# A hybrid decoder layer on one core: output ahead of the next joining, sample sums in a bank of their own, fewer DMAs in the inversion, embeddings projected by halves

## The chip, the cores and the metric

One Trainium2 chip, of which the kernel uses one core. The metric is device time in microseconds (us) of one execution. All times here are medians of repeated executions, or belong to the one execution that the profiler recorded.

## What is computed

One decoder layer is applied to a prompt of 1024 tokens and to 8 sequences of 8 tokens each ("the sample"), in float32.

```python
proj = x @ w_in                                   # token shift, RWKV-7 heads and gated-delta heads together
o_a = _rwkv7_mix(proj[..., :A_SHIFT_W], ...)      # 8 heads of 64
o_b = _gated_delta_mix(proj[..., A_SHIFT_W:], ...)# 4 heads of 128, chunks of 64
x = _layer_norm(DN_ALPHA * x + concat(o_a, o_b) @ w_o)
x = _layer_norm(DN_ALPHA * x + _conv_ffn(x))      # w_up (1024 x 5632), conv, silu, w_down (2816 x 1024)
e = _rms_norm(p @ w_ple)                          # per-layer input embeddings
x = x + sigmoid(x @ w_ple_gate) * e
```

Both mixers walk through the prompt in chunks. Within a chunk the recurrence becomes a triangular system (`triangular_solve(eye + Lmat, rhs)` in the reference for the gated-delta heads, the same in form for the RWKV heads), and a state is carried from chunk to chunk. The outputs are the two results and the new states.

## The kernel before

**Big products.** Every product with a weight matrix runs on TensorE (PE) in float32 that is split into two parts: `split` writes the rounded part `hi` on ScalarE (ACT) and the rest `lo` by a subtraction, on VectorE (DVE) or GpSimd (POOL) as its caller says. Three matmuls (hi·hi, hi·lo, lo·hi) of 128x512 add up in one PSUM bank. `wchunk` loads a weight chunk (`wraw`) and splits it into `whi` and `wlo`. There are three buffers of `whi`.

**Banks.** PSUM has 8 banks of 128x512. They are handed out by name: 4 `acc`, 2 `aux`, 2 `scan`. Within a name the banks go round in the order in which the program asks for them. A user that comes later in the program can't have a bank before the users ahead of it have had theirs. The four staging tiles `st` go round in the same way.

**Units.** Mixing is cut into 8 prompt units (half of the prompt `tb`, head group `g`, half of that `h`) and two sample units. A unit has five steps: `prep` (convolution, gates, the triangular matrices `MG` and `MB`), `invert`, `merge`, `scan` (the walk along the chunks, in the `scan` banks) and `mix_out`. `prep`, `merge` and `mix_out` use the `aux` banks.

**Inversion.** `invert` treats the 16x16 diagonal blocks of 24 systems of 64x64. Four DMAs write the matrices to DRAM (`inv_t`), four read the blocks back as 96 rows of 256 (`iN`), 28 short VectorE operations substitute into `iY`, two DMAs write the result and its transpose (`inv_x`, `inv_y`), and 16 read them back as `Dd` and `Dt`. All of these stand on the ACT engine's queue. `merge` then joins the blocks in four rounds of 64x64 matmuls. Each round opens with `touch`, a small matmul `aux<-zeros` that waits for the round's data, in the first two rounds for the DMAs of `Dt` and `Dd`. Behind it VectorE writes `DX` or `Y`.

**Order.** Instructions are put in order by the priority of their place in the program. What stands in `with s.fill()` has a lower priority and fills TensorE while a unit waits ("filler"): the projections of both halves (`proj`), the embeddings (`ple`), `w_o`, `w_up` and `w_down`. The first six column pairs of `proj(0)` stand ahead of `prep` of the first unit, pairs seven and eight (`next(pj)` twice) directly behind its `merge`. The loop over units runs `scan` of unit i with `merge` of unit i+1 woven into it (`ahead`), then `mix_out` of unit i, then `prep` of unit i+2.

**The sample in proj(0).** `proj_pair` multiplies each weight chunk with the prompt (two `acc` banks) and with the sample (a `scan` bank). `sfold` then transposes the sample's result in another `scan` bank and `store_sample` stores it, one pair late: ahead of `store_raw` of the pair that follows. `store_raw` is what empties that pair's two `acc` banks, through `st` tiles.

Of the kernel before, what the change touches and what calls it, by code (L numbers as in the profile page):

```python
# [16 lines left out]
D = 1024  # L17
# [128 lines left out]
class Kern:  # L146
    def __init__(s, ctx, tc, I, O):
        s.tc, s.nc, s.I, s.O = tc, tc.nc, I, O
        s.cp = ctx.enter_context(tc.tile_pool(name="const", bufs=1))
        s.mp = ctx.enter_context(tc.tile_pool(name="main", bufs=1))  # L150
        s.sp = s.mp
        s.ps = ctx.enter_context(tc.tile_pool(name="ps", bufs=4, space=PSUM))
        s.dp = ctx.enter_context(tc.tile_pool(name="dram", bufs=1, space=DRAM))
        s.bad, s.raw, s.rows, s.XW = {}, {}, {}, {}
        s.nbank = {"acc": 4, "aux": 2, "scan": 2}
        s.n = 0
        s.row = None
# [28 lines left out]
    def sbank(s):  # L186
        return s.bank("scan")

# [83 lines left out]
    def setup(s):  # L272
# [44 lines left out]
        for t in (s.Dd, s.Dt, *s.DX):  # L317
# [38 lines left out]
    def load_x(s, src, more=None):  # L356

        x = s.xtiles()
        if not more and not s.late:
            for k in range(0, KT, 2):  # L360
                raw = s.tl([128, D], "X", 3, dt=F32R, pool=s.c0).bitcast(F32).rearrange("p (k t) -> p k t", k=2)
                s.nc.sync.dma_start(raw, src[:, k:k + 2, :])
                s.split(x[k // 2][:, 0], x[k // 2][:, 1], raw, s.nc.vector if k < 4 else None)
            return x
        for k in range(KT):
            raw = s.hraw() if s.late else s.st()
            with s.tc.high_priority() if more and k < 1 else ExitStack():
                s.nc.sync.dma_start(raw, src[:, k, :])
                s.split(*s.xk(x, k), raw, s.nc.vector if more else None)
# [4 lines left out]
    def load_xs(s):  # L374
# [3 lines left out]
        def load(k):  # L378
            ks = slice(k, k + 2)
            s.nc.sync.dma_start(raw[:, ks], s.I["xT"][:, ks, T:T + 64])  # L380
            s.split(x[:, ks, 0, :], x[:, ks, 1, :], raw[:, ks], s.nc.vector)
# [3 lines left out]
    def wchunk(s, src, to=None):  # L385
# [4 lines left out]
        with s.tc.high_priority():  # L390
            s.nc.sync.dma_start(raw[:, :w], src)
            s.split(hi[:, :w], lo[:, :w], raw[:, :w], s.nc.vector)
        return hi, lo

    def proj_group(s, x, xs, wsrc, cuts, sample):

        acc = [s.bank("acc") for _ in cuts]
        sacc = s.sbank() if sample else None
# [42 lines left out]
    def sfold(s, pb, n):  # L441

        b = s.sbank()
# [9 lines left out]
    def proj(s, tb):  # L453
# [8 lines left out]
        if sample:  # L462
            s.store_sample(s.uad[:, 12:14], s.sfold(pb, 2), 2)
            q = s.sbank()
# [481 lines left out]

    def invert(s, sa, sb, small):

# [5 lines left out]
        dT = s.tl([64, 24, 64], "inv_t", 2, pool=s.dp)  # L954
        d1, d2 = (s.tl([96, 16, 16], t, 2, pool=s.dp) for t in ("inv_x", "inv_y"))
        N, Y, tmp = s.iN, s.iY, s.it
        DX = s.DX[0]
        s.DX = s.DX[::-1]
        for h, y, t in s.systems(sa, sb):
            s.uq.dma_start(dT[:, h * nh + y:h * nh + y + t.shape[1], :], t)  # L960
# [11 lines left out]
        s.uq.dma_start(d1[:n], Y[:n])  # L972
        if small:
            nc.gpsimd.memset(DX, 0.0)
            todo = ((DX, d1, 64),)
        else:
            nc.vector.tensor_copy(N[:n], Y[:n].rearrange("p c i -> p i c"))
            s.uq.dma_start(d2[:n], N[:n])
            todo = ((s.Dt, d2, 0), (s.Dd, d1, 0))
        for D, d, w in todo:  # L980
            for h in range(2):
                for k in range(4):
                    rows = slice(64 * h + 16 * k, 64 * h + 16 * k + 16)
                    cols = slice(w * h + 16 * k, w * h + 16 * k + 16)
                    y = k * ns + h * nh
                    if small:
                        s.uq.dma_start(D[rows, :2 * nch, cols], d[y:y + 2 * nch].rearrange("y r t -> r y t"))
                        if h == 0:
                            y += 2 * nch
                            s.uq.dma_start(D[rows, 8:8 + nb, cols], d[y:y + nb].rearrange("y r t -> r y t"))  # L990
                    else:
                        i = s.uq.dma_start(D[rows, :, cols], d[y:y + nh].rearrange("y r t -> r y t"))
                        sa.setdefault("dma", []).append(i.ins)
        sa["DX"] = sb["DX"] = DX

    def merge(s, sa, sb):
# [72 lines left out]
    def scan(s, tb, half, g, st, ahead):  # L1069
# [14 lines left out]
        s.together(a_all(), b_all(), *ahead)  # L1084
# [167 lines left out]
    def banks(s, alt):  # L1252
        return [s.bank(t) for t in (("aux", "aux", "scan", "scan") if alt else ("acc",) * 4)]
# [72 lines left out]
    def transposed(s, xs, i, c0, x, tag, dst=None):  # L1326
# [5 lines left out]
        for k in range(0, KT, q):  # L1332
# [19 lines left out]
            s.tt(lo, u, hi.bitcast(F32), ALU.subtract, s.nc.gpsimd if (k // q) % 2 else None)  # L1352
# [16 lines left out]
    def ple(s):  # L1369
        nc, I = s.nc, s.I  # L1370
        for tb in range(3):
# [12 lines left out]
            for h in range(2):  # L1384
# [6 lines left out]
                def evac(t, b):  # L1391
# [4 lines left out]
                s.dense(2, (lambda i: x[i]) if x else None, lambda i: I["w_ple"][h][:, i, :], evac,  # L1396
                        None if x else (lambda i: xs[:, i]), lambda v: out(8, 64, v))
# [211 lines left out]
    def run(s):  # L1609
# [124 lines left out]
```

## Time and profile before

| | |
|---|---|
| median of 3 runs | 1924.78 us (1918.24 to 1928.16) |
| the profiled execution | 1920.4 us, its span 1918.6 us |
| PE busy | 1831.8 us, 95% |
| DVE busy | 1269.8 us, 66% |
| ACT busy | 918.0 us, 48% |
| POOL busy | 154.7 us, 8% |
| mean granted TensorE clock | 0.989 of full speed |
| DMA | 255.88 MB, mean 133 GB/s |

Busy time counts what an engine executes; the issue of a DMA is not counted. The granted clock is one of two levels, 2.4 GHz (1.00) or 1.2 GHz; a stretch in between has some of each.

### The profile page before, as it was taken

Reading aid. Unit: us, or ns where it says so; the run is one execution under the profiler, and the core shown is the slowest. Engines: PE = TensorE matmul, PEld = TensorE weight load, DVE = VectorE, ACT = ScalarE, POOL = GpSimd, SP = SyncE. Lnnn points to the kernel's source line nnn. Section 1 sums busy time; section 2 is a strip of 40 time slices with the busy share of each in tenths; the row PEclk is TensorE's granted clock in tenths of the full one; section 3 lists DMA queues with packets and bytes.
Section 4 is the critical chain, followed back from the end, with each engine's and each line's share of the span. In section 5 each row is a group of like instructions: output and inputs, shape, how many; then the busy total and the mean of one; then the engine's idle time right before and its main releaser. Section 6 shows DMA issues by size and latency. Waiting matters only on the chain. (4 is left out here: it accounts for less than half of the span.)

```text
span 1918.6 us, 29879 instructions
## 1 busy us (share of the span) xinstructions
PE 1831.8 (95%) x10446; PEld 1463.3 (76%) x10446; DVE 1269.8 (66%) x2748; ACT 918.0 (48%) x1814; POOL 154.7 (8%) x305
## 2 busy tenths in 40 slices
PE   9999999999799798999999999999999999999998
PEld 7878777777567577777887767777787888888877
DVE  4366566758586685877768767666857752455488
ACT  5454447465564744646455435543633332333372
POOL 2000010001000000000000000200212210111000
PEclk9999999999899899999999999999999999999999
DMA  6435342434444365442423446875332222222355
GB/s 216 152 123 153 112 113 89 137 100 133 144 138 145 126 181 163 129 114 82 117 81 112 131 137 194 274 246 200 134 119 92 96 78 83 83 78 79 114 174 165
DMA packets 219126, 255.88 MB, mean 133 GB/s; under 512 B 81848, under 2 KB 117096, under 8 KB 218976
## 3 DMA queue, kind: packets, MB, share of 16 engines
q1 hardware_dynamic: 162040, 246.36, 39.8%
q10 hardware_dynamic: 56936, 7.62, 2.5%
q8 instruction: 82, 1.34, 0.3%
q14 instruction: 68, 0.56, 0.1%
HBM read 200.64 MB, written 53.26 MB: 132 GB/s over the span
## 5 line engine op out<-in xcount | busy, mean ns | idle before, releaser
L190 PE MATMUL acc<-x,whi 128*128 128x512 f32 x2400 | 784.5, 403 | 7.9 <-ACT whi L217 5.1
L220 DVE TENSOR_TENSOR wlo<-wraw,whi 128x512 fp32r<-128x512 f32 (+1 forms) x462 | 323.2, 700 | 343.7 <-ACT whi L217 319.0
L217 ACT ACTIVATE whi<-wraw 128x512 fp32r<-128x512 f32 (+1 forms) x462 | 287.4, 623 | 497.8 <-PE acc L190 169.0
L190 PEld LDWEIGHTS acc<-x,whi 128*128 128x128 f32 x2400 | 429.5, 189 | 89.0 <-issue 7.8
L190 PE MATMUL acc<-x,wlo 128*128 128x512 f32 x1200 | 483.0, 403 | 0.0
L190 PEld LDWEIGHTS acc<-x,wlo 128*128 128x128 f32 x1200 | 226.9, 189 | 54.3 <-issue 6.0
L190 PE MATMUL acc<-whi,X 128*128 128x512 f32 x436 | 145.5, 407 | 9.5 <-ACT st L217 6.2
L217 ACT ACTIVATE st<-acc 128x512 f32<-128x512 f32 (+2 forms) x134 | 77.4, 595 | 62.3 <-PE acc L190 39.2
L190 PEld LDWEIGHTS acc<-whi,X 128*128 128x128 f32 x436 | 81.9, 191 | 29.8 <-ACT st L217 7.2
L190 PE MATMUL acc<-wlo,X 128*128 128x512 f32 x220 | 87.5, 398 | 0.0
L229 DVE SCALAR_TENSOR_TENSOR st<-st,par,st 128x512 f32<-128x512 f32 (+1 forms) x132 | 78.1, 593 | 2.8
L217 ACT ACTIVATE st<-st 128x512 f32<-128x512 f32 x66 | 33.3, 505 | 72.9 <-DVE st L229 68.4
L190 PE MATMUL scan<-whi,X 128*128 128x256 f32 (+2 forms) x208 | 62.4, 335 | 0.0
L217 ACT ACTIVATE tmp<-tmp 128x512 f32<-128x512 f32 (+4 forms) x75 | 40.5, 548 | 30.6 <-DVE tmp L229 22.7
L229 DVE SCALAR_TENSOR_TENSOR st<-st,st 128x512 f32<-128x512 f32 x74 | 40.6, 550 | 19.5 <-ACT st L217 18.6
L190 PE MATMUL scan<-whi,xsm 128*128 128x256 f32 x176 | 49.3, 281 | 2.4 <-ACT st L217 2.4
L190 PE MATMUL scan<-wlo,X 128*128 128x256 f32 (+2 forms) x164 | 51.5, 314 | 0.0
L217 ACT ACTIVATE X<-wraw 128x512 fp32r<-128x512 f32 (+1 forms) x65 | 40.5, 623 | 21.1 <-DMA wraw<-hd 10.7
L506 POOL COPY tail<-st 128x3 f32<-128x3 f32 x52 | 14.6, 283 | 436.6 <-ACT st L217 436.6
L220 DVE TENSOR_TENSOR X<-wraw,X 128x512 fp32r<-128x512 f32 x60 | 43.5, 724 | 9.4 <-ACT X L217 9.3
L217 ACT ACTIVATE tmp<-tmp,par 128x256 f32<-128x256 f32 (+1 forms) x100 | 43.0, 470 | 14.0 <-issue 4.5
L190 PE MATMUL scan<-wlo,xsm 128*128 128x256 f32 x176 | 49.5, 282 | 0.0
(358 smaller groups left out, 3306.9 us busy)
## 6 DMA issues: line engine op xcount, KB each, us to landing
wraw<-w_up SPq DMA_DIRECT2D x176, 256.0 KB
wraw<-w_in SPq DMA_DIRECT2D x112, 256.0 KB
wraw<-w_down SPq DMA_DIRECT2D x98, 256.0 KB
wraw<-hd SPq DMA_DIRECT2D x44, 256.0 KB
wraw<-w_o SPq DMA_DIRECT2D x32, 256.0 KB
wraw<-w_gate SPq DMA_DIRECT2D x32, 256.0 KB
hd<-st SPq DMA_DIRECT2D x22, 256.0 KB
st<-lnv SPq DMA_DIRECT2D x20, 256.0 KB
```

The lines of the kernel that those rows point to most:

```text
L190: i = s.nc.tensor.matmul(out, lhsT=lhsT, rhs=rhs, start=start, stop=stop)
L217: s.nc.scalar.activation(out, in_, f, **kw)
L220: (eng or s.nc.vector).tensor_tensor(out, a, b, op)
L229: s.nc.vector.scalar_tensor_tensor(out, a, sc, b, op0, op1)
L506: s.nc.gpsimd.tensor_copy(s.tails[tb][:, f0 + f, :], st[:, TB - 3:TB])
```

## The change

1. **Order of the loop.** `merge` of unit i+1 is no longer woven into `scan` of unit i. It stands behind `mix_out` of unit i.
2. **Banks.** `acc` has 3 banks, and one bank is named `sum`. The sample's sums in `proj(0)` go to `sum`. Where there is no sample, `fbank` goes round over all four. `sfold` and the sample's gates in `proj(0)` take `aux` banks in place of `scan` banks.
3. **Inversion.** One DMA in place of four reads `iN`. The two results are written as 16x16 blocks on the diagonals of 64x64 systems in DRAM (`inv_dd`, `inv_dt`), in pieces of 64 bytes, and read as whole 64x64 systems with 4 DMAs in place of 16. The space beside the diagonal is set to zero once, by four DMAs at the start.
4. **Splits.** All subtractions of `split` and of the transposing splits run on VectorE, none on GpSimd.
5. **Embeddings.** The two weight chunks of a half are loaded first and kept, and the four token groups of 128 go in two halves, (0, 1) and (2, 3).

```diff
-        s.nbank = {"acc": 4, "aux": 2, "scan": 2}
+        s.nbank = {"acc": 3, "sum": 1, "aux": 2, "scan": 2}
+        s.turn = 0
...
+    def fbank(s, sample=False):
+        if sample:
+            return s.bank("acc")
+        s.turn = (s.turn + 1) % 4
+        return s.bank("acc" if s.turn else "sum")
...
-    def split(s, hi, lo, raw, eng=None):
+    def split(s, hi, lo, raw):
         s.act(hi, raw)
-        s.tt(lo, raw, hi.bitcast(F32), ALU.subtract, eng or s.nc.gpsimd)
+        s.tt(lo, raw, hi.bitcast(F32), ALU.subtract)
...
+        s.dd, s.dt = (s.tl([24, 65 * 64], t, pool=s.dp) for t in ("inv_dd", "inv_dt"))
+        for t in (s.dd, s.dt):
+            for h in range(2):
+                s.uq.dma_start(s.sysrows(t, slice(h, 24, 2)), s.DX[0][64 * h:64 * h + 64, :, 0:64])
...
     def proj_pair(s, x, xs, wsrc):
-        acc = [s.bank("acc") for _ in range(2)]
-        sacc = s.sbank() if xs is not None else None
+        early = xs is not None and not s.late
+        acc = [s.fbank(early) for _ in range(2)]
+        sacc = None if xs is None else s.bank("sum") if early else s.sbank()
...
     def sfold(s, pb, n):
-        b = s.sbank()
+        b = s.sbank() if s.late else s.bank()
...
+    def blocks(s, d, ns):
+        b = d.rearrange("y (k q) -> (y k) q", k=4)[:4 * ns, :16 * 64]
+        return b.rearrange("p (r l) -> p r l", l=64)[:, :, :16]
+
+    def sysrows(s, d, y):
+        return d[y, :64 * 64].rearrange("y (r t) -> r y t", t=64)
...
-        for k in range(4):
-            s.uq.dma_start(N[k * ns:(k + 1) * ns], dT[16 * k:16 * k + 16, :ns, 16 * k:16 * k + 16].rearrange("r y t -> y r t"))
+        s.uq.dma_start(N[:n], s.blocks(dT, ns))
...
-        s.uq.dma_start(d1[:n], Y[:n])
...
+            nc.vector.tensor_copy(N[:n], Y[:n].rearrange("p c i -> p i c"))
+            for X, d, D in ((N, s.dt, s.Dt), (Y, s.dd, s.Dd)):
+                s.uq.dma_start(s.blocks(d, ns), X[:n])
+                for h in range(2):
+                    i = s.uq.dma_start(D[64 * h:64 * h + 64], s.sysrows(d, slice(h, 24, 2)))
+                    sa.setdefault("dma", []).append(i.ins)
...
-                s.touch(bs[0], s.nc.cur_bb.bb.instructions[-1], *(sa["dma"][8 * k:8 * k + 8] if k < 2 else ()))
+                s.touch(bs[0], s.nc.cur_bb.bb.instructions[-1], *sa["dma"][2 * k:2 * k + 2])
...
-        s.together(a_all(), b_all(), *ahead)
+        s.together(a_all(), b_all())
...
-            s.tt(lo, u, hi.bitcast(F32), ALU.subtract, s.nc.gpsimd if (k // q) % 2 else None)
+            s.tt(lo, u, hi.bitcast(F32), ALU.subtract)
...
-                s.dense(2, (lambda i: x[i]) if x else None, lambda i: I["w_ple"][h][:, i, :], evac,
-                        None if x else (lambda i: xs[:, i]), lambda v: out(8, 64, v))
+                W = [s.wchunk(I["w_ple"][h][:, i, :]) for i in range(2)]
+                s.dense(2, (lambda i: x[i]) if x else None, None, evac, None if x else (lambda i: xs[:, i]),
+                        lambda v: out(8, 64, v), parts=((0, 1), (2, 3)) if x else ((),), kept=W)
...
-                    o = s.sample_scan(*u, st[i]) if len(u) == 1 else s.scan(*u, st[i], [s.merge(*st[i + 1][:2])] if len(units[i + 1]) == 3 else [])
+                    o = s.sample_scan(*u, st[i]) if len(u) == 1 else s.scan(*u, st[i])
...
                         s.mix_out(*u, st[i], o)
+                    if i + 1 < len(units) and len(units[i + 1]) == 3:
+                        for _ in s.merge(*st[i + 1][:2]):
+                            pass
```

**The first unit on TensorE.** Before, on PE, from the last transposes of `prep` (`aux_1290<-cst,tmp`) on, and further down at the first two rounds of `merge` (`acc` and `scan<-whi` or `wlo` are filler of `proj(0)`; `aux_1358` to `aux_1390` are `merge`):

```order
L214 MATMUL aux_1290<-cst_83,tmp_1243 128x128 x4
L190 MATMUL scan_2008<-whi_2032,X_135 128x256
L190 MATMUL scan_2008<-wlo_2033,X_135 128x256
L190 MATMUL acc_2006<-x_139,whi_2054 128x512 x2
...
L190 MATMUL acc_2225<-x_139,wlo_2273 128x512
L190 MATMUL aux_1358<-zeros_104 128x8
L190 MATMUL aux_1358<-Dt_120,MG_1188 64x64 x16
L190 MATMUL aux_1359<-Dt_120,MB_1265 64x64 x8
L190 MATMUL scan_2226<-whi_2272,X_135 128x256
...
L190 MATMUL aux_1389<-zeros_104 128x8
L190 MATMUL aux_1389<-Dd_119,DX_35_121 64x64 x16
```

After, on PE, the same stretch, from the same transposes (`aux_1294`) to the third round of `merge`, with nothing left out:

```order
L222 MATMUL aux_1294<-cst_83,tmp_1247 128x128 x4
L198 MATMUL aux_1345<-zeros_104 128x8
L198 MATMUL aux_1345<-Dt_120,MG_1192 64x64 x16
L198 MATMUL aux_1346<-Dt_120,MB_1269 64x64 x8
L198 MATMUL aux_1376<-zeros_104 128x8
L198 MATMUL aux_1376<-Dd_119,DX_35_121 64x64 x16
L198 MATMUL aux_1377<-Dd_119,DX_35_121 64x64 x8
L198 MATMUL aux_1405<-zeros_104 128x8
L198 MATMUL aux_1405<-Y_1343,DX_35_121 64x64 x16
```

No filler is left between the first unit's `prep` and the end of its `merge`. Counted over the whole order, the rows from the transposes `aux<-tmp,cst` at the start of the first unit's triangular matrices to the last product of `merge` hold 162 filler matmuls of 512 columns and 54 of 256 before, and none after. After, the next filler stands here, at the end of `merge` (`aux_1478`), where the transposes of `sfold` (`aux_1577`, `aux_1684`) come too:

```order
L198 MATMUL aux_1478<-DX_35_121,Y_1465 128x64 x4
L222 MATMUL aux_1577<-cst_83,st_991 128x128 x2
L222 MATMUL aux_1684<-cst_83,st_1575 128x128 x2
L198 MATMUL scan_3964<-RB_3943,DX_35_121 128x128 x2
L198 MATMUL acc_1592<-x_141,whi_1595 128x512 x2
```

**The start on ScalarE.** Before, on ACT, the first rows of the program (`x_137<-st_148` is the second of the input's eight chunks):

```order
L217 ACTIVATE x_137<-st_141 128x512
L217 ACTIVATE whi_190<-wraw_189 128x320
L217 ACTIVATE whi_207<-wraw_206 128x320
L217 ACTIVATE whi_224<-wraw_223 128x320
L217 ACTIVATE X_135<-tmp_136 128x2x64
L217 ACTIVATE x_137<-st_148 128x512
```

After, on ACT, the same rows (`x_141<-st_152` is the second chunk):

```order
L330 DMA inv_dd_125<-DX_35_121 64x12x64
L225 ACTIVATE x_141<-st_145 128x512
L225 ACTIVATE whi_194<-wraw_193 128x320
L225 ACTIVATE whi_211<-wraw_210 128x320
L225 ACTIVATE whi_228<-wraw_227 128x320
L225 ACTIVATE X_139<-tmp_140 128x2x64
L330 DMA inv_dd_125<-DX_35_121 64x12x64
L330 DMA inv_dt_126<-DX_35_121 64x12x64
L225 ACTIVATE whi_245<-wraw_244 128x320
L330 DMA inv_dt_126<-DX_35_121 64x12x64
L225 ACTIVATE x_141<-st_152 128x512
```

The four zeroing DMAs and one weight chunk now stand ahead of the second chunk.

**Output and the next joining on TensorE.** Before, on PE, at the end of the first unit's `scan`: the second unit's `merge` (`aux_4146` to `aux_4185`) comes first, and the first unit's output (`aux_4254<-OA`) behind it.

```order
L214 MATMUL aux_4146<-cst_83,DX_36_122 128x128 x4
...
L190 MATMUL aux_4165<-Y_4145,MB_1915 128x64 x4
...
L190 MATMUL aux_4185<-DX_36_122,Y_4145 128x64 x4
...
L190 MATMUL scan_4238<-UV_1190,BT_1189 128x128
L190 MATMUL acc_2686<-x_2668,wlo_2795 128x512
L190 MATMUL acc_2687<-x_2668,whi_2794 128x512
L190 MATMUL aux_4254<-OA_3960,cst_83 128x512
```

After, on PE, the output (`aux_4083` to `aux_4101`) comes first, and the second unit's `merge` opens behind it with `aux_4115<-zeros`:

```order
L198 MATMUL aux_4083<-OA_3930,cst_83 128x512
...
L198 MATMUL aux_4088<-otmp_4081,cst_83 128x512
L198 MATMUL aux_4092<-otmp_4082,cst_83 128x512
...
L198 MATMUL aux_4101<-SG_1064,g_14_86 128x256 x2
L198 MATMUL aux_4115<-zeros_104 128x8
L198 MATMUL aux_4115<-Dt_120,MG_1826 64x64 x16
```

`merge` no longer lies beside `scan`, and the output no longer waits for the `aux` banks that `merge` holds.

## Rows read from the trace of the kernel before

**Rows 1.** Page, part 1: busy time and share of the span by engine.

```profile
PE 1831.8 (95%) x10446; PEld 1463.3 (76%) x10446; DVE 1269.8 (66%) x2748; ACT 918.0 (48%) x1814; POOL 154.7 (8%) x305
```

**Rows 2.** Windows: us, busy (count) of PE, PEld, DVE, ACT, POOL, clock, DMA.

```profile
120.00:200.00 80.00, 79.68 (x587) 65.48 (x587) 54.74 (x131) 38.30 (x81) 2.32 (x8) 1.00 0.47 141
200.00:600.00 400.00, 367.56 (x2459) 292.95 (x2458) 282.11 (x672) 227.80 (x465) 24.23 (x44) 0.98 0.40 123
600.00:760.00 160.00, 140.89 (x1014) 112.41 (x1012) 103.35 (x236) 75.26 (x147) 3.65 (x9) 0.94 0.51 157
```

**Rows 3.** Windows with the granted clock (the 0.5 to 0.6 column) low, columns as in rows 2.

```profile
486.00:494.00 8.00, 4.44 (x54) 4.11 (x55) 2.09 (x4) 1.93 (x4) 0.00 (x0) 0.57 0.34 60
520.00:528.00 8.00, 6.42 (x24) 5.62 (x25) 7.26 (x17) 6.14 (x16) 0.00 (x0) 0.57 0.49 178
640.00:651.00 11.00, 8.53 (x28) 5.88 (x29) 5.88 (x11) 9.59 (x18) 0.00 (x0) 0.53 0.53 171
674.00:681.00 7.00, 6.35 (x32) 5.39 (x32) 6.55 (x15) 0.90 (x2) 0.00 (x0) 0.51 0.76 198
```

**Rows 4.** Timeline of PE, five long waits: start, length, in brackets the wait before.

```profile
489.56 0.34 PE L190 MATMUL aux<-zeros 128*128 128x8 f32 x1 [8.37 <-DMA Dt<-inv_y]
...
521.58 1.22 PE L190 MATMUL acc<-whi,X 128*128 128x512 f32 x2 [5.16 <-ACT st L217]
...
638.38 1.10 PE L190 MATMUL aux<-tmp,cst 128*128 128x512 f32 x2 [2.54 <-DVE otmp L220]
...
672.74 1.12 PE L190 MATMUL aux<-tmp,cst 128*128 128x512 f32 x2 [3.76 <-DVE tmp L229]
...
745.41 0.24 PE L190 MATMUL aux<-zeros 128*128 128x8 f32 x1 [2.36 <-DMA raw_v<-st]
```

**Rows 5.** Timeline of PE, first unit from triangular matrices to the end of merge.

```profile
136.09 1.12 PE L190 MATMUL aux<-tmp,cst 128*128 128x512 f32 x2
...
152.75 0.62 PE L190 MATMUL acc<-x,whi 128*128 128x512 f32 x2
...
154.38 0.62 PE L190 MATMUL acc<-x,whi 128*128 128x512 f32 x2
...
182.14 0.17 PE L190 MATMUL aux<-zeros 128*128 128x8 f32 x1
...
198.12 1.11 PE L190 MATMUL aux<-DX,Y 128*128 128x64 f32 x8
```

**Rows 6.** Windows of the first unit: inversion, then merge; columns as in rows 2.

```profile
152.70:182.10 29.40, 29.40 (x148) 24.82 (x148) 20.10 (x62) 14.37 (x30) 0.84 (x3) 1.00 0.47 136
182.10:199.20 17.10, 17.10 (x256) 14.72 (x256) 8.54 (x16) 5.38 (x11) 0.56 (x3) 1.00 0.32 96
```

**Rows 7.** Timeline of DVE, first unit: start and end of the substitution.

```profile
161.25 0.28 DVE L964 COPY iY<-iN 96x256 f32<-96x256 f32 x1
...
171.63 0.38 DVE L977 COPY iN<-iY 96x256 f32<-96x256 f32 x1
```

**Rows 8.** Timeline of ACT's DMA queue, first unit: its writes and reads.

```profile
152.91 0.58 ACTq L960 DMA_DIRECT2D inv_t<-MB  x1
...
156.29 1.88 ACTq L963 DMA_DIRECT2D iN<-inv_t  x4
...
172.15 0.32 ACTq L978 DMA_DIRECT2D inv_y<-iN  x1
...
174.00 2.54 ACTq L992 DMA_DIRECT2D Dt<-inv_y  x3
...
176.69 1.90 ACTq L992 DMA_DIRECT2D Dt<-inv_y  x4
```

**Rows 9.** Tile inv_y: the reads of Dt over the program, ns min/median/max.

```profile
L992 ACTq DMA_DIRECT2D Dt<-inv_y x64: 309/449/1635, 174.0 to 957.9; - x64
```

**Rows 10.** Timeline of ACT at the start of the program.

```profile
7.57 1.29 ACT L217 ACTIVATE x<-st 128x512 fp32r<-128x512 f32 x2 [0.79 <-DMA st<-xT]
```

**Rows 11.** Group of POOL by line: count, busy us and mean ns, idle before.

```profile
L220 POOL TENSOR_TENSOR hl<-st,hh 128x512 fp32r<-128x512 f32 x22 | 29.1, 1324 | 99.1 <-ACT hh L217 99.1
```

More of the change, by code (lines that the diff above doesn't have):

```diff
@@ L316, in setup @@
         s.DX = [s.tl([128, 12, LB], "DX%d" % i) for i in range(2)]
-        for t in (s.Dd, s.Dt, *s.DX):
+        for t in s.DX:
             nc.gpsimd.memset(t, 0.0)
+        s.dd, s.dt = (s.tl([24, 65 * 64], t, pool=s.dp) for t in ("inv_dd", "inv_dt"))
+        for t in (s.dd, s.dt):
+            for h in range(2):
+                s.uq.dma_start(s.sysrows(t, slice(h, 24, 2)), s.DX[0][64 * h:64 * h + 64, :, 0:64])
         for g in range(2):
@@ L362, in load_x @@
                 s.nc.sync.dma_start(raw, src[:, k:k + 2, :])
-                s.split(x[k // 2][:, 0], x[k // 2][:, 1], raw, s.nc.vector if k < 4 else None)
+                s.split(x[k // 2][:, 0], x[k // 2][:, 1], raw)
             return x
@@ L368, in load_x @@
                 s.nc.sync.dma_start(raw, src[:, k, :])
-                s.split(*s.xk(x, k), raw, s.nc.vector if more else None)
+                s.split(*s.xk(x, k), raw)
                 if more and k % 2 == 0:
@@ L391, in wchunk @@
             s.nc.sync.dma_start(raw[:, :w], src)
-            s.split(hi[:, :w], lo[:, :w], raw[:, :w], s.nc.vector)
+            s.split(hi[:, :w], lo[:, :w], raw[:, :w])
         return hi, lo
     def proj_group(s, x, xs, wsrc, cuts, sample):
-        acc = [s.bank("acc") for _ in cuts]
-        sacc = s.sbank() if sample else None
+        acc = [s.fbank(sample) for _ in cuts]
+        sacc = s.bank("sum") if sample else None
         w = wsrc.shape[-1]
@@ L463, in proj @@
             s.store_sample(s.uad[:, 12:14], s.sfold(pb, 2), 2)
-            q = s.sbank()
+            q = s.bank()
             for i in range(2):
@@ L953, in invert @@
         ns = nh + (2 * nch if small else nh)
-        dT = s.tl([64, 24, 64], "inv_t", 2, pool=s.dp)
-        d1, d2 = (s.tl([96, 16, 16], t, 2, pool=s.dp) for t in ("inv_x", "inv_y"))
+        dT = s.tl([24, 65 * 64], "inv_t", 2, pool=s.dp)
         N, Y, tmp = s.iN, s.iY, s.it
@@ L958, in invert, with of @@
         s.DX = s.DX[::-1]
+        def of(h, y, n):
+            return slice(h * nh + y, h * nh + y + n) if small else slice(2 * y + h, 2 * (y + n) + h - 1, 2)
         for h, y, t in s.systems(sa, sb):
-            s.uq.dma_start(dT[:, h * nh + y:h * nh + y + t.shape[1], :], t)
+            s.uq.dma_start(s.sysrows(dT, of(h, y, t.shape[1])), t)
         n = 4 * ns
-        for k in range(4):
-            s.uq.dma_start(N[k * ns:(k + 1) * ns], dT[16 * k:16 * k + 16, :ns, 16 * k:16 * k + 16].rearrange("r y t -> y r t"))
+        s.uq.dma_start(N[:n], s.blocks(dT, ns))
         nc.vector.tensor_copy(Y[:n], N[:n])
@@ L971, in invert @@
         nc.vector.memset(Y[:n].rearrange("p a b -> p (a b)")[:, 0::17], 1.0)
-        s.uq.dma_start(d1[:n], Y[:n])
         if small:
+            d = s.tl([96, 16, 16], "inv_x", 2, pool=s.dp)
+            s.uq.dma_start(d[:n], Y[:n])
+            d = d.rearrange("(y k) r t -> k r y t", k=4)
             nc.gpsimd.memset(DX, 0.0)
[L975 to L980, printed above, removed]
             for h in range(2):
@@ L983, in invert @@
                     rows = slice(64 * h + 16 * k, 64 * h + 16 * k + 16)
[L984 to L993, printed above, removed]
+                    y = h * nh
+                    s.uq.dma_start(DX[rows, :2 * nch, rows], d[k, :, y:y + 2 * nch, :])
+                    if h == 0:
+                        s.uq.dma_start(DX[rows, 8:8 + nb, rows], d[k, :, 2 * nch:nh, :])
+        else:
+            nc.vector.tensor_copy(N[:n], Y[:n].rearrange("p c i -> p i c"))
[4 more added lines that the diff above has]
+                    sa.setdefault("dma", []).append(i.ins)
         sa["DX"] = sb["DX"] = DX
@@ L1067, in prep, with scan @@
         return sa, sb, Z
-    def scan(s, tb, half, g, st, ahead):
+    def scan(s, tb, half, g, st):
         sa, sb, Z = st
@@ L1252, in banks @@
     def banks(s, alt):
-        return [s.bank(t) for t in (("aux", "aux", "scan", "scan") if alt else ("acc",) * 4)]
+        return [s.bank(t) for t in (("aux", "aux", "scan", "scan") if alt else ("acc", "acc", "acc", "sum"))]
     def dense(s, n, act, wsrc, evac, xs=None, sevac=None, alt=False, parts=((0, 1, 2, 3),), kept=None, ahead=None):
```

2 lines of the change are left out of this document (1 added, 1 removed).

## The prediction

> **What bounds the kernel now.** I read the page's busy times first. TensorE works for 1831.8 us, 95% of the span, VectorE for 66% and ScalarE for 48% [rows 1]. No matmul is removed, so the time can change only where TensorE waits or where its clock falls. The windows show where that is. From 120 to 200 us, which holds the first unit's inversion, PE is busy for 79.68 of 80 us. From 200 to 600 it lacks 32.4 us, and from 600 to 760 19.1 us [rows 2]. Those 51.5 us are the waits that the change can reach. The granted clock adds to them: in four short stretches of 8, 8, 11 and 7 us it averages 0.57, 0.57, 0.53 and 0.51, which means the 1.2 GHz level for most of each [rows 3]. What it costs there is length times (1 - clock): 3.4 + 3.4 + 5.2 + 3.4 = 15.4 us. So 67 us lie open between 200 and 760.
>
> The timeline names the larger waits [rows 4]: 8.37 us for the DMA of Dt (the second round's data of an inversion), 5.16 us for ScalarE's emptying of `acc` banks in the embeddings, 2.54 us in an output step behind the joining, 3.76 us and 2.36 us in preparation. All but the last stand in or just ahead of a stretch with the low clock [rows 3, 4].
>
> **The first unit: what the change takes away.** This is the largest term, and it speaks against the change. Before, PE is never idle from the triangular matrices (136.09) to the end of the first joining (198.12 plus 1.11) [rows 5]: the inversion from 152.7 to 182.1 shows 29.40 busy of 29.40 us, the joining 17.10 of 17.10 [rows 6]. All of the inversion's 29.4 us is filler, since PE has nothing of the unit to do until `aux<-zeros` at 182.14 [rows 5].
>
> In the changed order that filler is gone. The reason lies in the banks. `sfold` of the sixth column pair now asks for an `aux` bank, and asks for it behind the eight `aux` banks of the first `merge`, so it can't have one before `merge` is through. The `st` tile of its result comes ahead of those that empty two `acc` banks, so these stay full. With three `acc` banks only one more sum can be formed, then all filler stands still. Before, `sfold` had a `scan` bank and went on.
>
> The price: 162 matmuls of 512 and 54 of 256 columns are missing there, by the count of the order. A group of six and two takes 1.63 us (152.75 to 154.38) [rows 5], so 27 such groups are 44 us of work that PE now does later, while it idles here. From the 44 comes off what the stretch itself gets shorter. It is 199.2 - 136.1 = 63 us long [rows 5]. Without filler PE answers at once. One DMA reads `iN`, where four take 1.88 us to issue [rows 8]. The substitution, which takes 10.4 us from 161.25 to 171.63 [rows 7], has less beside it on VectorE. And four reads follow the write in place of sixteen (the seven of Dt shown take 2.54 and 1.90 us [rows 8]). I put this at 8 us together, between 2 and 16: at 2 the chain on VectorE and the DMAs' landing set everything, at 16 all of PE's queueing in preparation goes too. An idle engine also comes back at 1.2 GHz: each stretch in rows 3 that follows a long wait costs 3.4 to 5.2 us, so +4. The term is 44 - 8 + 4 = **+40 us**, between 28 and 47.
>
> **The inversion's DMAs.** The results are now written as 1536 pieces of 64 bytes. The nearest rows: the write in rows of 1 KB, issued at 172.15, is read from 174.00 on, 1.85 us later; the read of 1536 pieces of 64 bytes begins at 156.29 and its data is used at 161.25, 4.96 us later [rows 7, 8]. I take about 4 us for such a write, some 2 more than now, which eats a part of what fewer reads give. It is inside the 8 us above.
>
> The Trainium skill speaks against such writes (page "DMA: Bandwidth & Descriptors", section "Specifications"): a transfer wants at least 512 bytes for the full rate, and below that the DMA engine reads, changes and writes back. The trace shows 64-byte pieces only as reads, so no run here shows that for writes yet; by the page the write would lie at or above the 4.96 us of the read, and my sum would be 1 us or more higher.
>
> On ScalarE 15 DMA issues fewer per unit, at 0.449 us (median) [rows 9], are 6.7 us per unit, 54 us over eight. ScalarE is busy for 48% [rows 1], so it counts only through the waits below.
>
> **The later units: what it gives.** The output no longer waits for the `aux` banks of a `merge` whose inversion is still on the way; it now runs during that inversion. That should take away the 2.54 us wait and the slow stretch around 640 to 651 that goes with it (5.2 us). The wait of 8.37 us with its 3.4 us goes if Dt lands earlier and 44 us more filler are at hand. The wait of 5.16 us with its 3.4 us goes with the embeddings in halves, where two banks are emptied while two are filled. Together 28 us. The waits of 3.76 and 2.36 us are in preparation, which isn't changed; I leave them. So **-28 us**, between -10 (only the output's) and -45 (two thirds of the 67).
>
> What is late next: `merge` was woven into `scan`, and the two filled each other's gaps on PE. Now they stand one behind the other, with filler between. VectorE has 282 of 400 us in this stretch [rows 2] and gets the splits too. I add **+6 us**, between 0 and 15.
>
> **Small terms.** At the start, four zeroing DMAs and one weight chunk stand on ScalarE ahead of the second chunk of the input, which it now converts at 7.57 [rows 10]. Four issues at 0.449 us [rows 9] are 1.8 us: **+2**, between 0 and 4, as one of them may wait for another transfer. Three `acc` banks and one `sum` bank in `proj(0)`: the sum must be emptied before the next pair's sample products: **+1**, 0 to 4. The splits off GpSimd: 22 of 1324 ns each [rows 11] and a few of that kind behind transposes become VectorE work of about half the length; where PE waits for them that is worth **-1**, -4 to +2.
>
> Sum: 40 - 28 + 6 + 2 + 1 - 1 = +20 us. The profiled execution took 1920.4 us, 4.4 less than the median of 1924.8. So 1940 against the profiled one, and **1945 us** against the median.
>
> **The rivals.** 0.5% is 9.6 us, about what a measurement here can tell from no change.
>
> *The later filler pays it all back.* The 44 us of filler are moved, not added, and 67 us are open between 200 and 760. If most of those were only want of filler and late outputs, 60 us would go: 40 + 2 + 1 - 1 - 60 = -18, **1907 us**. It decides from 52 us removed on. For it: the two longest waits are both of that kind. Against it: many waits in preparation and scan are single small ones, where TensorE waits for VectorE or ScalarE, and filler was there before too.
>
> *The hole is small.* With the term at 28 (the chain gets shorter by 16 us, since VectorE and ScalarE have little else to do) and 33 removed: 28 + 2 + 1 - 1 - 33 + 6 = +3, **1928 us**. For it: VectorE is busy for 20.1 of the 29.4 us of the inversion, a good part with filler's splits [rows 6]. Against it: the joining's own steps alternate between PE and VectorE and can't overlap.
>
> *The small writes are slow everywhere.* If each 64-byte write takes 8 us in place of 4, the first unit pays 4 more, and the waits for Dt stay (8.37 + 3.4 not removed): 1945 + 16 = **1961 us**. By the Trainium skill (same page, section "Specifications") this is the likelier; rows speak of reads only.
>
> **How the numbers follow.** The forecast has 0.45, the later filler 0.25, the small hole 0.2, the slow writes 0.1. Forecast and slow writes end slower, so 0.55 slower, 0.2 within 0.5%, 0.25 faster. The likeliest is 1945 us, by its own bounds 1930 to 1962. The range reaches from 1905, just below the later filler's time, to 1970.
>
> **What would show it.** In the new trace PE should stand idle for 20 us or more in one wait ahead of the first `aux<-zeros` of a joining near 150 to 180 us, with a low clock behind it, and the 80 us from 120 on should show some 40 less busy. The first joining should end at about the same time or up to 16 us earlier. Later, the wait for Dt near 490, the one near 521 and the slow stretch near 640 should be gone. The prediction is wrong if PE works through the first inversion, or if the waits between 200 and 760 fall from 51.5 to under 10 us.

## The result, and the profile after

The changed kernel takes 1952.58 us (median of 4 runs, 1947.4 to 1955.49), the kernel before 1925.96 us beside it. The medians differ by 26.6 us (1.4%). The estimated ratio is 1.0155, with a 95% interval of 1.0131 to 1.0178: slower by 1.55%. The profiled execution spans 1953.4 us, 34.8 more than that of before.

On the page TensorE is busy for 12.9 us longer than in [rows 1], with the same matmuls and a lower mean granted clock (0.971, before 0.989), and so idle for 21.9 us longer:

```profile
PE 1844.7 (94%) x10446; PEld 1480.7 (76%) x10446; DVE 1282.3 (66%) x2824; ACT 921.8 (47%) x1816; POOL 57.2 (3%) x227
```

The windows of the same stretches as in [rows 2], and one more (columns: us, busy and count of PE, PEld, DVE, ACT, POOL, clock, DMA):

```profile
120.00:200.00 80.00, 47.57 (x372) 38.47 (x371) 47.64 (x120) 29.21 (x57) 0.00 (x0) 0.69 0.26 69
200.00:600.00 400.00, 386.76 (x2579) 310.03 (x2579) 267.98 (x627) 230.14 (x469) 11.12 (x38) 0.99 0.46 134
600.00:760.00 160.00, 147.12 (x920) 117.36 (x919) 111.03 (x275) 86.63 (x167) 4.00 (x13) 0.96 0.58 168
760.00:1130.00 370.00, 344.34 (x2324) 268.32 (x2323) 279.34 (x752) 195.98 (x422) 12.79 (x42) 0.96 0.40 111
```

From 120 to 200 us TensorE lost 32.1 us of busy time. Between 200 and 760 it waits for 13.2 + 12.9 = 26.1 us, where it was 51.5. Between 760 and 1130 it waits for 25.7 us, where it was 10.0 (370 less 360.05 busy).

The timeline of PE shows the first unit, beside [rows 5] (in brackets the wait ahead of the instruction):

```profile
143.61 2.07 PE L198 MATMUL aux<-tmp,cst 128*128 128x512 f32 x2 [2.62 <-DVE tmp L237]
...
183.78 0.34 PE L198 MATMUL aux<-zeros 128*128 128x8 f32 x1 [23.68 <-DMA Dt<-inv_dt]
...
188.43 0.35 PE L198 MATMUL aux<-zeros 128*128 128x8 f32 x1 [1.56 <-issue]
...
206.06 1.10 PE L198 MATMUL aux<-DX,Y 128*128 128x64 f32 x8 [0.41 <-ACT Y L225]
```

The clock in that stretch, by windows: 0.77, 0.58 and 0.60 (the eighth column), around a wait in which PE is busy for 0.32 of 24 us.

```profile
130.00:160.00 30.00, 24.57 (x132) 19.40 (x128) 22.55 (x48) 13.38 (x30) 0.00 (x0) 0.77 0.36 112
160.00:184.00 24.00, 0.32 (x2) 0.26 (x1) 14.58 (x54) 6.72 (x14) 0.00 (x0) 0.58 0.32 54
184.00:210.00 26.00, 21.91 (x247) 20.15 (x248) 7.93 (x16) 4.12 (x12) 0.00 (x0) 0.60 0.03 12
```

The start, on ScalarE (its DMA queue too): the second chunk of the input is converted at 11.22 us, where it was 7.57 [rows 10]. The weight chunk ahead of it waits 1.83 us for PE, and the chunk itself another 1.18.

```profile
8.85 0.61 ACTq L330 DMA_DIRECT2D inv_dt<-DX  x1
9.57 0.47 ACT L225 ACTIVATE whi<-wraw 128x320 fp32r<-128x320 f32 x1 [1.83 <-PE sum L198]
10.59 0.58 ACTq L330 DMA_DIRECT2D inv_dt<-DX  x1
11.22 1.15 ACT L225 ACTIVATE x<-st 128x512 fp32r<-128x512 f32 x2 [1.18 <-DMA wraw<-w_g]
```

### The profile page after: what moved, and what is told of

Its sections match the earlier page's. It is cut to its first block, busy times and chain, and to the rows that moved or that the text cites. A ratio compares the mean times of both kernels' runs of the same rounds, so it can differ in the third digit from the quotient of the medians.

```text
span 1953.4 us, 29625 instructions
## 1 busy us (share of the span) xinstructions
PE 1844.7 (94%) x10446; PEld 1480.7 (76%) x10446; DVE 1282.3 (66%) x2824; ACT 921.8 (47%) x1816; POOL 57.2 (3%) x227
## 5 line engine op out<-in xcount | busy, mean ns | idle before, releaser
L198 PE MATMUL acc<-x,whi 128*128 128x512 f32 x1936 | 636.4, 405 | 13.5 <-ACT whi L225 4.8
L198 PEld LDWEIGHTS acc<-x,whi 128*128 128x128 f32 x1936 | 351.3, 190 | 84.9 <-issue 7.8
L198 PE MATMUL acc<-x,wlo 128*128 128x512 f32 x968 | 388.7, 403 | 0.0
L198 PEld LDWEIGHTS acc<-x,wlo 128*128 128x128 f32 x968 | 183.8, 190 | 41.4 <-issue 2.1
L198 PE MATMUL sum<-x,whi 128*128 128x512 f32 x464 | 152.2, 403 | 0.5 <-ACT whi L225 0.5
L198 PE MATMUL sum<-x,wlo 128*128 128x512 f32 x232 | 93.1, 401 | 0.0
L198 PEld LDWEIGHTS sum<-x,whi 128*128 128x128 f32 x464 | 81.0, 189 | 15.9 <-issue 3.0
L198 PE MATMUL sum<-whi,X 128*128 128x256 f32 (+2 forms) x228 | 71.2, 350 | 3.5 <-DVE st L237 3.0
L198 PEld LDWEIGHTS acc<-whi,X 128*128 128x128 f32 x328 | 60.8, 189 | 12.4 <-issue 0.2
L198 PE MATMUL sum<-wlo,X 128*128 128x256 f32 (+2 forms) x174 | 56.3, 324 | 0.0
L225 ACT ACTIVATE tmp<-tmp,par 128x256 f32<-128x256 f32 (+1 forms) x100 | 42.9, 470 | 23.4 <-DVE tmp L237 9.2
L198 PEld LDWEIGHTS sum<-x,wlo 128*128 128x128 f32 x232 | 43.8, 189 | 10.5 <-issue 1.0
```

The lines of the kernel that those rows point to most:

```text
L198: i = s.nc.tensor.matmul(out, lhsT=lhsT, rhs=rhs, start=start, stop=stop)
L225: s.nc.scalar.activation(out, in_, f, **kw)
```

## The experiments

**1. Is it the folding behind the joining's banks?** The changed kernel with one edit:

```diff
     def sfold(s, pb, n):
-        b = s.sbank() if s.late else s.bank()
+        b = s.sbank()
...
-            q = s.bank()
+            q = s.sbank()
```

> The changed kernel, with the folding of the sample's sums and the sample's gates in the scan banks again; nothing else. Theory (the folding queues behind the first joining's aux banks and stops all filler): its order has 143 filler matmuls of 512 columns in the first unit again, the wait of 23.7 us ahead of the first joining and the low clock around it go, and of the changed kernel's 1953 us some 36 go: 1917 us, between 1908 and 1927. Rival (three acc banks, or the sum bank, are what stops the filler): the wait stays at 15 us or more and the time within 6 us of 1953.

Measured: 1924.26 us, 28.3 less than the changed kernel; ratio to before 1.0001 (0.9985 to 1.0016). Its windows, with a clock of 0.96 in the first:

```profile
120.00:200.00 80.00, 74.54 (x410) 58.36 (x409) 51.73 (x126) 41.47 (x84) 2.52 (x6) 0.96 0.49 144
200.00:600.00 400.00, 375.22 (x2624) 298.00 (x2623) 288.08 (x696) 235.99 (x476) 13.77 (x36) 0.98 0.45 127
600.00:760.00 160.00, 146.28 (x1049) 116.63 (x1047) 102.84 (x232) 82.11 (x156) 3.37 (x11) 0.96 0.58 172
```

The wait ahead of the first joining is 4.11 us in place of 23.68. So the place of `sfold` decides, and the rival with the three `acc` banks falls. The gain is 28 us where 36 were expected. The windows also show what the hole had given back: without it TensorE waits for 24.8 + 13.7 = 38.5 us between 200 and 760, with it for 26.1. The filler that the hole pushed back covered 12.4 us of later waits. (These are single executions; experiments 3 and 4 give 11.8 for the same pair of kernels, 38.8 less 27.0.)

**2. The same edit alone, on the kernel before.**

```diff
     def sfold(s, pb, n):
-        b = s.sbank()
+        b = s.sbank() if s.late else s.bank()
...
-            q = s.sbank()
+            q = s.bank()
```

> The kernel before, with nothing but the folding and the sample's gates moved to the aux banks; four acc banks, woven joining, sixteen reads stay. Theory: the hole opens here too, with 11 filler matmuls of 512 columns left in it: 1926 + 33 = 1959 us, between 1945 and 1970, and a wait of 15 us or more ahead of the first joining. Rival (the filler that is moved is paid back later, since the kernel before has 51.5 us of waits between 200 and 760 us): 1926 to 1938 us.

Measured: 1953.77 us, ratio 1.0140 (1.0117 to 1.0163), 28.2 us more than before. The timeline of PE has the hole, with four `acc` banks and the old reads:

```profile
176.68 0.35 PE L190 MATMUL aux<-zeros 128*128 128x8 f32 x1 [23.09 <-DMA Dd<-inv_x]
```

Between 200 and 760 us TensorE waits for 33.5 us in this kernel, 18.0 less than before: the hole pays back here too. Put in or taken out, the edit moves the time by 28 us. That is about as much as the whole change loses; its other parts together come out at nothing.

**3. The zeroing at the start.** The changed kernel, zeroing from GpSimd's queue:

```diff
-                s.uq.dma_start(s.sysrows(t, slice(h, 24, 2)), ...)
+                nc.gpsimd.dma_start(s.sysrows(t, slice(h, 24, 2)), ...)
```

> The changed kernel, with the four zeroing DMAs of the start issued from GpSimd's queue in place of ScalarE's; the start of ScalarE's order is then that of before. Theory (the zeroing DMAs hold up the second chunk of the input): PE's waits of 1.8 and 3.1 us near 12 to 15 us and the low clock up to 20 us go, 1953 - 9 = 1944 us, between 1940 and 1948. Rival (the start is late for the bytes of the zeroing, whichever queue issues them): 1950 to 1956 us.

Measured: 1947.23 us, 5.4 less than the changed kernel (ratio to before 1.0103, 1.0081 to 1.0126). Up to 20 us the changed kernel has PE busy for 10.32 us at a clock of 0.84, this one for 15.40 us at 1.00, as the kernel before (15.41). The gain is inside the expected range, at its small end. The first unit's `aux<-tmp,cst`, at 143.61 us in the changed kernel, starts at 135.97 here. The queue that issues the DMAs decides, not their bytes. It isn't the issuing alone: the four issues in the changed kernel take 2.46 us together. Its order on VectorE differs too. Operations on the parameters (`par`) stand there ahead of the second chunk's subtraction and wait 3.80 us for their DMA; in this run they stand behind it:

```profile
14.36 0.17 DVE L243 TENSOR_SCALAR omu<-par 128x14 f32<-128x14 f32 x1 [3.80 <-DMA par<-par]
...
14.73 1.28 DVE L228 TENSOR_TENSOR x<-st,x 128x512 fp32r<-128x512 f32 x2
```

PE waits 3.06 us for that subtraction, and 1.81 us for ScalarE's conversion of the same chunk.

**4. Both together.**

> Both edits, folding in the scan banks and zeroing from GpSimd's queue. If the two losses are separate: 1953 - 36 - 9 = 1908 us, between 1898 and 1920, faster than before (1926). Rival (a wait that the hole covered comes out, such as the one near 800 us where VectorE is busy 14.5 of 15 us): 1920 to 1935 us, no faster than before.

Measured: 1917.35 us, ratio 0.9951 (0.9932 to 0.9971). Against experiment 1 the zeroing is worth 6.9 us here. The two losses are separate: 35 us go with both edits, 28 and 5 with one of them. What is left of the change gives only 8 us.

**5 to 8. Four parts of the change, each alone on the kernel before.** The loop's order:

```diff
-   o = ... s.scan(*u, st[i], [s.merge(*st[i + 1][:2])] if len(units[i + 1]) == 3 else [])
+   o = ... s.scan(*u, st[i], [])
...
        s.mix_out(*u, st[i], o)
+   if i + 1 < len(units) and len(units[i + 1]) == 3:
+       for _ in s.merge(*st[i + 1][:2]):
+           pass
```

> The kernel before, with nothing but the order of the loop changed: output of a unit, then the joining of the next, not woven into the scan. Theory of the prediction (late outputs cause the waits between 200 and 760 us): 1926 - 20 = 1906 us, between 1898 and 1912. Rival (what fell there in the changed kernel was paid by the filler that the hole had moved; weaving and output first are worth about the same): 1920 to 1934 us.

Measured: 1924.91 us, ratio 1.0012 (0.9987 to 1.0037). The rival's range holds the time. The order does what it says: the last output is stored at 1125.3 us, where it was 1182.4, and the wait of 2.54 us for `otmp` [rows 4] is gone. That alone buys nothing: between 200 and 760 us TensorE is idle for 51.7 us, where it was 51.5, since other waits came, the longest 7.26 us for Dd and 6.36 us for ScalarE's `st`.

The inversion's DMAs, with `blocks`, `sysrows` and `invert` as in the change (so `inv_t`, too, is laid out as whole systems), zeroing from GpSimd:

> The kernel before, with nothing but the inversion's DMAs changed (one read of iN, results in pieces of 64 bytes, four reads), the zeroing from GpSimd's queue. Theory (Dt lands earlier, the wait of 8.37 us near 489 and its low clock go): 1926 - 8 = 1918 us, between 1913 and 1922. Rival (writes in pieces of 64 bytes are slow, Dt lands no earlier): 1924 to 1934 us.

Measured: 1945.93 us, ratio 1.0114 (1.0068 to 1.0161). Neither expected a loss of this size. In the first unit the DMA queue of ScalarE shows 4.96 us from the issue of the write to the first read of Dt, where [rows 8] have 1.85:

```profile
172.25 0.31 ACTq L1004 DMA_DIRECT2D inv_dt<-iN  x1
...
177.21 1.30 ACTq L1006 DMA_DIRECT2D Dt<-inv_dt  x2
```

TensorE waits for Dt for 23.0 us in all, 4 times, 12.9 more than before. The rest of the loss isn't pinned down: more waits are spread over the mixing, whose order is another one in many places.

The embeddings in halves and the splits on VectorE, each as in the change:

> The kernel before, with nothing but the embeddings' projection in two halves with kept weights. Theory (the wait of 5.16 us near 521 for the emptying of banks and its low clock go): 1926 - 8 = 1918 us, between 1914 and 1922. Rival (the wait is ScalarE being late with a unit's own work, and stays): 1923 to 1930 us.

> The kernel before, with nothing but all splits on VectorE. Theory (the changed kernels lose some 18 us less between 1130 and 1400 us, where GpSimd's 1.3 us subtractions stand): 1926 - 12 = 1914 us, between 1908 and 1920. Rival (VectorE gets fuller in the mixing, and the late part's gain is the loop's order): 1924 to 1936 us.

Measured: 1924.27 us (0.9997, 0.9973 to 1.0021) and 1919.75 us (0.9983, 0.9959 to 1.0007). The first is no change. Its wait does go: between 200 and 760 us PE's waits for `st` ahead of `acc` fall from 6.6 to 0.4 us. But the waits for Dt and Dd there grow from 10.1 to 19.6, of which this one was not there before:

```profile
613.94 0.35 PE L190 MATMUL aux<-zeros 128*128 128x8 f32 x1 [7.54 <-DMA Dd<-inv_x]
```

The second is unclear; by the medians it is 5.6 us, about half of what its theory said. The 18 us of that theory aren't in the windows: from 1130 to 1400 the changed kernel is idle for 4.6 us (265.41 of 270 busy), where it was 10.2.

**9. The changed kernel with the folding mended and the old inversion.** `invert`, the two first rounds' waits in `merge`, and `setup` as before:

```diff
-        s.uq.dma_start(N[:n], s.blocks(dT, ns))
+        for k in range(4):
+            s.uq.dma_start(N[k * ns:(k + 1) * ns], dT[16 * k:16 * k + 16, :ns, ...])
...
-                s.uq.dma_start(s.blocks(d, ns), X[:n])
+        s.uq.dma_start(d1[:n], Y[:n])    # rows of 1 KB; d2 likewise; sixteen reads as before
```

> The changed kernel with the folding in the scan banks and the inversion's DMAs as before (no zeroing, rows of 1 KB written, four reads of iN, sixteen of Dd and Dt); the loop's order, the banks, the splits and the embeddings stay changed. Theory (the new DMAs land Dt later, since writing in 64-byte pieces costs more than twelve reads fewer give back; the run with both mended but the new DMAs took 1917 us and waits 13.0 us for Dt): 1917 - 8 = 1909 us, between 1900 and 1914. Rival (54 us less of DMA issues on ScalarE were worth something in the changed order): 1918 to 1928 us.

Measured: 1911.46 us, ratio 0.9921 (0.9905 to 0.9937). The time is the theory's: the new DMAs cost 5.9 us in this order (against experiment 4; the two intervals leave some 5 us either way), although ScalarE issues 15 fewer per unit. Its path holds for the first unit alone, where PE waits 3.75 us for Dt with the new DMAs and not at all with the old. Later it is the other way round: between 200 and 760 us PE waits 3.9 us for Dt and Dd with the new ones and 13.3 with the old. What came in place of those are waits for ScalarE's `st` ahead of `acc`, 8.2 us with the new DMAs and 0.3 with the old.

**10. The same with the joining woven in again.**

```diff
-                    o = ... s.scan(*u, st[i])
+                    o = ... s.scan(*u, st[i], [s.merge(*st[i + 1][:2])] if len(units[i + 1]) == 3 else [])
```

> As the run with the old inversion, but with the joining woven into the scan as before, output behind it; banks, splits and embeddings stay changed. If the loop's order is worth nothing, as it was on the kernel before alone: within 5 us of that run. If it needs the other parts to give something: 8 us or more slower than it.

Measured: 1943.35 us, ratio 1.0097 (1.0078 to 1.0117), 31.9 us more than experiment 9. So the loop's order gives 32 us beside the other parts, and nothing beside none of them. The new banks are among these parts: that the woven joining goes badly with three `acc` banks is a rival that no run separates, since splits and embeddings were not run with the woven order and the old banks. The last output comes at 1205.6 us, 78.7 later than in experiment 9 (1126.9).

**11. Pieces of 64 bytes alone, on the kernel before.**

```diff
-        d1, d2 = (s.tl([96, 16, 16], t, 2, pool=s.dp) for t in ("inv_x", "inv_y"))
+        d1, d2 = (s.tl([96, 16, 32], t, 2, pool=s.dp)[:, :, :16] for t in ("inv_x", "inv_y"))
```

> The kernel before, with nothing but the two results of the inversion written to DRAM rows of 128 bytes, of which 64 are used, so in 1536 pieces of 64 bytes in place of 96 of 1 KB; the sixteen reads take pieces of 64 bytes as before, and no zeroing is needed. Theory (the small pieces make the write late): from its issue to the first read of Dt 4 to 5 us in place of 1.9 in the first unit, the waits for Dt grow from 10.1 to 18 us or more, and the time is 1926 + 12 = 1938 us, between 1931 and 1948. Rival (other things made the new DMAs late, such as the 64x64 reads): 1921 to 1930 us.

Measured: 1946.67 us, ratio 1.0106 (1.0086 to 1.0125). The time lies in the expected range, but 21 us are lost where 12 were expected, and the path is another one: from the write to the first read of Dt it is 3.49 us (172.11 to 175.60), and the DMA waits on TensorE grow only to 14.9 us, all for Dd. The order of this kernel, too, is another one in many places. That small pieces make the write late is shown, by the other result too: from the write of `inv_x` to the first read of Dd it is 3.13 us (171.27 to 174.40), before 1.94 (171.62 to 173.56). How much of the 21 us is that, and how much the new order, isn't settled.

```profile
171.27 0.64 ACTq L972 DMA_DIRECT2D inv_x<-iY  x1
172.11 0.82 ACTq L978 DMA_DIRECT2D inv_y<-iN  x1
...
174.40 0.86 ACTq L992 DMA_DIRECT2D Dd<-inv_x  x2
175.60 1.68 ACTq L992 DMA_DIRECT2D Dt<-inv_y  x2
```

The same two lines of `inv_x` before:

```profile
171.62 0.33 ACTq L972 DMA_DIRECT2D inv_x<-iY  x1
...
173.56 0.32 ACTq L992 DMA_DIRECT2D Dd<-inv_x  x1
```

**12. As experiment 9, with the banks of before.** What is left of the change is the loop's order, the splits and the embeddings.

```diff
-        s.nbank = {"acc": 3, "sum": 1, "aux": 2, "scan": 2}
+        s.nbank = {"acc": 4, "aux": 2, "scan": 2}
...
-        return s.bank("acc" if s.turn else "sum")
+        return s.bank("acc")
...
-        sacc = s.bank("sum") if sample else None
+        sacc = s.sbank() if sample else None
...
-        sacc = None if xs is None else s.bank("sum") if early else s.sbank()
+        sacc = None if xs is None else s.sbank()
...
-        return [s.bank(t) for t in (("aux", "aux", "scan", "scan") if alt else ("acc", "acc", "acc", "sum"))]
+        return [s.bank(t) for t in (("aux", "aux", "scan", "scan") if alt else ("acc",) * 4)]
```

> As the run with the folding in the scan banks and the old inversion (1911 us), but with four acc banks and no sum bank, so that the loop's order, the splits and the embeddings are all that is left of the change. If the sum bank gives something of its own: 1917 us, between 1915 and 1922. If it gives nothing, and the loop's order with the other two is the whole gain: 1906 to 1914 us.

Measured: 1902.17 us, ratio 0.9864 (0.9842 to 0.9885). It beats both kernels, and both expectations: the new banks (three `acc` and one `sum`) cost 9.3 us (again with some 5 us either way). The loss lies between 760 and 1130 us, where TensorE waits for 22.9 us in experiment 9 and for 13.0 here. The window of experiment 9:

```profile
760.00:1130.00 370.00, 347.13 (x2196) 265.95 (x2197) 283.29 (x755) 189.23 (x403) 14.00 (x45) 0.97 0.38 111
```

One place is seen in the timelines of PE. Where the first layer norm's transposes (`acc<-cst,X`) meet a unit's preparation, PE in experiment 9, with three `acc` banks, waits like this:

```profile
770.35 2.08 PE L198 MATMUL aux<-tmp,cst 128*128 128x512 f32 x2 [7.02 <-DVE tmp L237]
```

With four, in experiment 12, like this:

```profile
759.33 2.08 PE L198 MATMUL aux<-tmp,cst 128*128 128x512 f32 x2 [1.02 <-DVE tmp L237]
```

The changed kernel has the same wait at 810.57, 7.67 us, behind which its clock falls to 0.50 from 815 to 822. Why three banks let the two meet is not shown.

The windows of experiment 12 stand beside [rows 2]; the last two of them had 360.05 and 259.78 us busy before:

```profile
200.00:600.00 400.00, 370.64 (x2459) 297.26 (x2458) 285.90 (x691) 232.56 (x470) 11.09 (x34) 0.96 0.43 123
600.00:760.00 160.00, 147.71 (x1085) 116.62 (x1084) 116.87 (x262) 93.37 (x185) 3.37 (x11) 0.98 0.54 165
760.00:1130.00 370.00, 356.98 (x2235) 275.71 (x2234) 278.41 (x745) 187.23 (x401) 16.54 (x47) 0.97 0.39 112
1130.00:1400.00 270.00, 264.98 (x1190) 213.41 (x1189) 179.20 (x295) 125.44 (x206) 2.02 (x9) 1.00 0.65 204
```

Put in a row, the medians make a ladder from the best version to the changed kernel: 1902.2, + 9.3 for the new banks = 1911.5, + 5.9 for the inversion's DMAs = 1917.4, + 6.9 for the zeroing on ScalarE = 1924.3, + 28.3 for the folding = 1952.6. Each step is one part put back on the ones before it; in another sequence the steps would differ. The kernel before, run beside each of them, took 1925.1 to 1926.8 us, and the intervals leave each of the three smaller steps open by some 5 us either way.

## Why the prediction was right, and where its terms were not

**The first unit** was forecast as the largest term, with its mechanism: `sfold` behind the `aux` banks of the first joining. Experiments 1 and 2 show it from both sides. They measure 28.3 and 28.2 us against the +40, just inside the lower bound of 28. That bound is 44 - 16, without the +4 for the clock; with it, it would be 32. Three parts of the term were off. The stretch did not get 8 us shorter: from `aux<-tmp,cst` to the end of the joining it took 63.6 us (143.61 to 206.06 plus 1.10), and 63.1 before. Its inversion did get shorter, with 23.68 us of waiting in place of 29.4. But the joining took 23.4 us (183.78 to 207.16) in place of 17.1. In slices of 3 us the clock is 0.50 in each from 183 to 204; in experiment 2, where it is back at 1.00 from 180 to 192, the joining takes 17.9 (176.68 to 194.58). Up to the fourth `aux<-zeros`, where both kernels do the same, it is 11.93 against 9.58; behind it, first steps of the scan lie in between in the changed kernel. By that the clock cost between 2 and 5 us, an estimate not far from the +4. And the filler was partly paid back: 12.4 us of later waits went (18.0 in experiment 2), which the forecast put down to the loop's order. By these numbers the term is 44 - 12.4 = 31.6 against 28.3 measured. That 40 - 12 comes out nearer is luck, since the 8 us taken off the 44 did not come.

The joining also ended 8 us later than before (207.16 against 199.2), where it was to end at the same time or earlier. The stretch began 7.5 us later (143.61 against 136.09), which is the start's loss: with the zeroing on GpSimd's queue it begins at 135.97 (experiment 3).

**The start**, +2, was mis-sized: 5.4 to 6.9 us. I counted four issues at 0.449 us; these take 2.46 us. In the trace the second chunk comes 3.65 us later on ScalarE (11.22 to 7.57), with a wait of its weight chunk for PE in between. VectorE takes up the chunk only at 14.73 us, behind its 3.80 us wait for `par`. Behind that PE runs with the clock at 0.50 from 16 to 20 us. I had counted neither.

**The sum bank**, +1, was mis-sized: 9.3 us in experiment 12, beyond its bound of 4. I had looked at the first projection alone. The wait that is seen with it stands in the first layer norm, where `acc` banks serve transposes.

**The later units**, -28 and +6, came out at about the right size for the wrong reason. Three parts (order, splits, embeddings) give 24.6 us in experiment 12, where I had -28 + 6 - 1 = -23. But the step failed that took the length of each named wait as the time its removal gives. The named waits do go, and others come in their place. The 2.54 us for `otmp` is there, to the hundredth, in the kernel before and in experiments 6, 7, 8, 10 and 11, all woven, and in no run with the new order; yet the order alone gives nothing (experiment 5). (Experiment 2, woven but with the hole, lacks it too.) The wait for `st` in the embeddings goes with the halves, and the waits for Dt and Dd grow by more (experiment 7). The wait for Dt or Dd near 490 has several causes. With the old inversion it is still 8.59 us in experiment 9 and 9.22 in experiment 12. With the new DMAs in the changed order it is 1.6 and 1.7 us in experiments 1 and 4, without any hole, but on the kernel before it is 11.77 (experiment 6). The hole alone, on the kernel before, brings it to 4.34 (experiment 2, at 517). So more filler and the new DMAs both shorten it there, as the forecast said, but not on every kernel, and the total did not follow.

Alone the three parts sum to some 7 us by their medians, none of them clear of the noise; together they give 24.6. That they need each other is shown, but not by which chain; experiment 10 has the new banks beside the order and can't tell. The profile shows only where: idle time between 200 and 760 falls from 51.5 to 41.7 us, and from 1130 to 1400 from 10.2 to 5.0. These are two executions whose spans differ by 17.3 us.

The 15.4 us that the prediction put on the low clock between 200 and 760 were too much. It multiplied the whole length of each stretch by (1 - clock), but PE is idle for part of it [rows 3], and that part already stands in the 51.5. By the busy times it is 1.9 + 2.8 + 4.0 + 3.1 = 11.8 us.

**The inversion's DMAs** were put inside the 8 us as a gain that small writes eat in part. They eat all of it: 5.9 us lost in the changed order, 20 us on the kernel before. My 4 us for such a write was near: 3.6 us in the changed kernel (175.37 to 178.97), 4.96 in experiment 6, 3.49 in experiment 11. What I missed is that four reads in place of sixteen return little in the first unit: in the changed kernel the last read of Dt is issued by 180.27, and PE starts at 183.78, 3.5 us later. The rule of the Trainium skill (page "DMA: Bandwidth & Descriptors", section "Specifications"), that pieces below 512 bytes lose rate and are read, changed and written back, points the right way: 3.49 us against 1.85 for the same bytes. That it is the reading back that costs, no run here shows.

**The rivals.** The later filler did pay back, but 12 to 18 us and not 60. The small hole's number came out, 28, but not its reason: the chain did not get 16 us shorter. Slow small writes were real, at 3.5 to 5 us and not 8, and beside the hole, not in place of it. That the sum came out near (+20 forecast, some 27 measured) owes something to errors of both signs: the hole 12 too high, start, sum bank and DMAs together about 18 too low.

## What to carry to other kernels

When an operation moves to another pool of buffers that are handed out in program order, look at what stands ahead of it in that pool, and at everything that queues behind it; here a transpose of two small tiles, waiting for a bank, stopped all filler for 24 us. A change made of several parts can be a sum of gains and losses: the same change without its new banks and DMAs is 1.4% faster than before, with them 1.55% slower, so take it apart before it is kept or dropped. Parts that give nothing clear alone can be worth 25 us together, so undo them one by one from the whole too, not only add them one by one to the start. And the length of a wait is not the time that its removal gives: look in the next trace for the waits that come in its place.

## What the runs showed of the hardware

The same 96 KB written to DRAM in 64-byte pieces could be read by the next DMA later than in rows of 1 KB: the first read came 3.13 us after the issue of the write in place of 1.94 for `inv_x`, and 3.49 in place of 1.85 for `inv_y` (experiment 11, and before [rows 8]). Four zeroing DMAs issued at the start from the queue of ScalarE, which also feeds TensorE, cost 5.4 and 6.9 us (experiments 3 and 4), with another order on VectorE as part of it. Issued from GpSimd's queue they leave PE busy for 15.40 of the first 20 us, where it is 15.41 without them. After the 23.68 us wait the granted clock stayed at 0.50 from 183 to 204 us, while PE was busy for 16.8 of these 21 us. In experiment 2, after a wait of 23.09 us and ahead of the same products, it was back at 1.00 from 180 to 192. What decides between the two is not shown.
